# A streaming-encoder block with a retrieval layer: larger portions for the sort that runs beside the u stage, and an earlier load of the last bias row by ScalarE

## The chip, the cores and the metric

The kernel runs on one core of a Trainium2 chip. The metric is device time in microseconds. Engines: TensorE (PE), VectorE (DVE), ScalarE (ACT), GpSimd (POOL) and SyncE (SP); each works through its own queue in order. DMAs are issued by SyncE, ScalarE and GpSimd, and 16 DMA engines serve them all.

## The reference, cut to what matters

One layer over 256 positions of width 2048: adaLN modulation, a mixer (convolution and latent attention), and a retrieval layer, after which the result is scaled by a gate, added and normalised. The part around the change is the retrieval layer:

```python
scores = einsum('bshpd,hpnd->bshpn', q, sub_keys)
top_v, top_i = top_k(scores, 16)                  # per head and half
best_v, best_i = top_k(top_v[0] + top_v[1], 16)
expert = i1 * 128 + i2                            # one of 128*128 experts
gate = softmax(best_v)
act = gelu(einsum('td,tnd->tn', h, u_tab[expert])) * gate
x = x + gt_f * einsum('tn,tnd->td', act, v_tab[expert])
y = rms_norm(x)                                   # gt_f = silu(c) @ W_ada[5] + b_ada[5]
```

Each of 256 positions picks 128 of 16384 experts.

## The kernel before, in words

The first third of the program is the modulation, the mixer and the query projection. Then come two stages for the retrieval layer.

**The u stage** goes through all 16384 experts in 128 blocks of 128 (the loop `for i1 in range(NBLK)`). For a block SyncE loads 1 MB of u (`ru`, L214); ScalarE copies it to a rounded high part `hu` (L225), VectorE makes the low part `lu` as the difference (L226), and TensorE does 32 products with `hu` (L241, L242) and then 16 with `lu` (L247). There are two buffers for `hu` and `lu` and four for `ru`. ScalarE takes Gelu of the result into a tile `A` of eight blocks (L1269).

Beside it, "side" work is handed out in portions. A generator yields, after each piece of work, a number that stands for its cost; `pay(x)` adds `x` to a budget at each block and takes pieces until the budget is spent. Up to block 49 the side work is the choice of experts: one-hot products that write the gate of each expert and position to the DRAM tensor `gd`. From block 50 on it is `sort_steps`: experts of 128 at a time are sorted by which groups of positions use them. Its steps in order: a mask and two keys (VectorE, tile `work`), 24 classes, their counts (`clstot` on TensorE), prefix sums and the flag `miss`, then six times four classes: ranks (`rank`, TensorE, L1145 and L1148) and their collection (`rk`, L1133, L1138, L1140), then the place of each expert (`place`, cast at L1164). Then GpSimd issues 128 scatters (L1170), which write the experts' names to their places in DRAM (`permd`), loads them back (L1180) and casts them to `perm_idx` (L1183).

Four more things run in the u stage. Every fourth to eighth block `ask` loads the gates `gg` (L1203), `weigh` multiplies them into `A` (L1209, VectorE) and `put` stores the product to `actd` (L1213). `gtf_steps` sums the last modulation row from sixteen 1 MB loads (L1055, L1057); in block 118 `gtf_finish` adds its rows up on TensorE (`gtfp`, L1066) and adds the bias row `bt` on VectorE (L1067). Right behind it VectorE works out `half_rows` from `perm_idx` (L1315). In blocks 108 to 124 (`EARLY_AT`) GpSimd issues nine gathers of v rows by `perm_idx` (`early`, `rv`; L1238). Block 125 stores the last part of the activations.

**The tail.** GpSimd gathers v rows (1 MB each) and the activations that belong to them (`mc`, `mcs`; L1249), 109 of each, and TensorE multiplies them (`po`, L1323) in an order that `plan()` lays down; some need high and low parts (L230, L231). At the end VectorE and ScalarE scale by `gtf`, add and normalise.

What sets the order: `bt` and the `gg` tiles share a pool of two buffers (`g8`). `keep` holds an instruction in program order on its engine; elsewhere the scheduler places instructions by dependence and priority. So a piece of side work that is handed out in an earlier block stands earlier in its engine's queue.

Of the kernel before, what the change touches and what calls it, by code (L numbers as in the profile page):

```python
# [28 lines left out]
NBLK = 128  # L29
# [21 lines left out]
DEFER = (15, 16, 17, 18, 19)  # L51
SORT_FROM = 51
SORT_SIDE = 2.4
TAIL = 2
HELD = 5
AHEAD = 14
# [97 lines left out]
def hybrid_block_kernel(  # L154
# [22 lines left out]
    nc = tc.nc  # L177
    V, S, PE = nc.vector, nc.scalar, nc.tensor
# [11 lines left out]
    def ps_tile(name):  # L190
        return psp.tile([128, 512], F32, tag="ps", name=name)
# [16 lines left out]
    def keep(x):  # L208
        tc.keep_in_program_order(x)
        return x  # L210
# [6 lines left out]
    def load_split(src, name, hp=HPP, alloc=None):  # L217
        raw = load_raw(src, "r" + name)
        with tc.high_priority(offset=hp):
            if alloc is not None:  # L220
                hi, lo = alloc("h" + name), alloc("l" + name)
            else:
                hi = wp.tile([128, 2048], F32R, tag="whi", name="h" + name)
                lo = wp.tile([128, 2048], F32R, tag="wlo", name="l" + name)
            S.activation(hi, raw, AF.Copy)  # L225
            V.tensor_tensor(lo, raw, hi.bitcast(F32), ALU.subtract)  # L226
        return hi, lo
# [5 lines left out]
    def mm3(dst, w, rhs, ncx, woff=0, sets=None):  # L233
        whi, wlo = w
        rhi, rlo = rhs
        sets = sets or (tuple(range(ncx)),)
        last = sets[-1][2:] + sets[-1][:2] if isinstance(rhi, Behind) else sets[-1]
        for cs in sets:
            for c in cs:
                sl = slice((woff + c) * 128, (woff + c + 1) * 128)  # L240
                PE.matmul(dst, lhsT=whi[:, sl], rhs=rhi[:, c], start=(c == sets[0][0]), stop=False)  # L241
                PE.matmul(dst, lhsT=whi[:, sl], rhs=rlo[:, c], start=False, stop=False)  # L242
            if isinstance(rhi, Behind):
                cs = cs[2:] + cs[:2]
            for c in cs:
                sl = slice((woff + c) * 128, (woff + c + 1) * 128)
                PE.matmul(dst, lhsT=wlo[:, sl], rhs=rhi[:, c], start=False, stop=(c == cs[-1] and cs == last))  # L247
# [626 lines left out]
    def a8(name, shape=(128, 8, 256), dt=F32):  # L874
        return ap_.tile(list(shape), dt, tag="A", name=name, bufs=ABUFS)

    def g8(name, shape, dt=F32):
        return gp.tile(list(shape), dt, tag="G", name=name)
# [12 lines left out]
    def e2(name):  # L891
        return sp.tile([128, 512], F32, tag="e2", name=name, bufs=E2BUFS)
# [157 lines left out]
    def gtf_steps(acc):  # L1050
        for k in range(16):
            raw = load_raw(w_ada[3, k], f"ada5_{k}")
            yield
            if k == 0:
                keep(V.tensor_scalar(acc, raw, cact[:, 0:1], None, ALU.mult))  # L1055
            else:
                keep(V.scalar_tensor_tensor(acc, raw, cact[:, k:k + 1], acc, ALU.mult, ALU.add))  # L1057
            yield

    def gtf_finish(acc):  # L1060
        bt = g8("bt", (128, 2048))
        nc.gpsimd.dma_start(bt, b_gtf.partition_broadcast(128))
        for j in range(4):
            p = ps_tile(f"gtfp{j}")
            sl = slice(j * 512, (j + 1) * 512)
            PE.matmul(p, lhsT=ones, rhs=acc[:, sl], start=True, stop=True)  # L1066
            V.tensor_tensor(acc[:, sl], p, bt[:, sl], ALU.add)  # L1067
# [121 lines left out]
    def pay(x):  # L1189
        nonlocal budget  # L1190
        budget += x
        while budget > 0:
            st = next(side, None)
            if st is None:
                break
            budget -= st
# [4 lines left out]
    def ask(k):  # L1201
        gg = ggs[k] = g8(f"gg{k}", (128, T // TB, ABLK, TB))
        keep((S if 1 < k < NG - 1 else nc.gpsimd).dma_start(gg, gd[:, :, k * ABLK:(k + 1) * ABLK, :].rearrange("tb p i t -> p tb i t")))  # L1203

    def weigh(k, n=ABLK):
        gg = ggs.pop(k)
        av = ab[k].rearrange("p i (a t) -> p i a t", t=TB)
        gv = gg.rearrange("p a i t -> p i a t")
        keep(V.tensor_tensor(av[:, :n], av[:, :n], gv[:, :n], ALU.mult))  # L1209
        return av, gv  # L1210

    def put(k, n):
        keep((S if k else nc.gpsimd).dma_start(actd[k * ABLK * 128:(k * ABLK + n) * 128].rearrange("(i p) t -> p i t", p=128),  # L1213
                                ab[k][:, :n]))
# [27 lines left out]
    def fetch_m(m):  # L1242
        n = len(ms)
        to, at, rows = m, actd[:, :], index(ORDER[n])
        for h in range(2):
            if not need[n] >> 4 * (1 - h) & 15:
                to, at = m[:, 128 * h:128 * h + 128], actd.rearrange("r (h t) -> (r h) t", h=2)
                rows = bass.IndirectOffsetOnAxis(ap=half_rows[h][:, ORDER[n]:ORDER[n] + 1], axis=0)
        keep(nc.gpsimd.indirect_dma_start(to, None, at, rows))  # L1249
        ms.append(m)  # L1250

    def fetch_early():
        n = len(raws)
        if n == 0:
            t2.append(cst.tile([128, 2, 2048], F32, tag="T2", name="early"))
        if n < 2:
            fetch_raw("T2", t2[0][:, n])
        elif n == 7:
            fetch_raw("R", g8(f"rv{n}", (128, 2048)))
        else:  # L1260
            fetch_raw("R", a8(f"rv{n}", (128, 2048)))

    for i1 in range(NBLK):
        if i1 % ABLK == 0:
            ab.append(a8(f"A{i1}"))
        w = load_split(peer_u[i1], f"u{i1}", HPU)
        p = ps_tile(f"pu{i1}")
        mm3(p[:, :256], w, h2, 16)
        S.activation(ab[-1][:, i1 % ABLK], p[:, :256], AF.Gelu)  # L1269
        if i1 < UPART:  # L1270
            pay(SIDE)
            continue
        if i1 == UPART:
            for _ in side:
                pass
            gtf = sp.tile([128, 2048], F32, tag="tk", name="gtf")
            gts = gtf_steps(gtf)
            side = sort_steps()
            budget = 0.0
        for k in weighs.get(i1 - 1, ()):  # L1280
            if k:
                put(k, ABLK)
        for k in weighs.get(i1, ()):
            weigh(k)
            if not k:
                put(k, ABLK)
        for k in asks.get(i1, ()):
            ask(k)
        if i1 == EARLY_AT[0]:
            for _ in side:  # L1290
                pass
        if i1 in EARLY_AT:
            fetch_early()
        if i1 == NBLK - TAIL - 1:
            last = weigh(NG - 1, ABLK - TAIL)
            put(NG - 1, ABLK - TAIL)
            for k in range(4):
                pair = e2(f"mc{k}")
                m_free.extend((-1, pair[:, 256 * j:256 * j + 256]) for j in range(2))
            for _ in range(4):  # L1300
                fetch_m(m_free.pop(0)[-1])
        if i1 >= NBLK - TAIL:
            r = i1 % ABLK
            keep(V.tensor_tensor(last[0][:, r], last[0][:, r], last[1][:, r], ALU.mult))
        if i1 >= SORT_FROM:
            pay(SORT_SIDE)
        if i1 % 2 == 0:
            next(gts, None)
        if i1 == NBLK - 10:
            for _ in gts:  # L1310
                pass
            gtf_finish(gtf)
            half_rows = [x.bitcast(U32) for x in (ident, ones)]
            for h in range(2):
                keep(V.tensor_scalar(half_rows[h], perm, 2.0, float(h), ALU.mult, ALU.add))  # L1315
# [251 lines left out]
```

## Time and profile before

| what | value |
|---|---|
| time, median of 3 runs | 1705.12 us (1704.20 to 1711.65) |
| profiled execution, its time and its span | 1709.15 us, 1707.2 us |
| PE, DVE, ACT, POOL busy | 95%, 65%, 41%, 29% |
| mean granted clock of TensorE | 0.983 |
| the u stage, first `lu` product to last | 556 to 1335 us |
| scatters | 994.0 to 1261.3 us |
| DMA, mean over the span | 295 GB/s |

How to read the rows: a timeline row has the start, the duration, the engine, the line, the operation, the tile written and the tiles read, and in brackets the idle time of the engine before it with what ended it. A row of waits has who waited for whom: the total, the number of times, the longest. A row of windows has for one stretch the busy time of PE, PEld (TensorE's weight load), DVE, ACT and POOL with the instructions in brackets, then the granted clock, the DMA share and GB/s.

### The profile page before, as it was taken

How to read it: one execution, taken by the hardware profiler on the slowest of the kernel's cores; microseconds unless marked ns; L12 is line 12 of the kernel's file. 1: busy time of each engine (PE TensorE's matmuls, PEld its weight loads, DVE VectorE, ACT ScalarE, POOL GpSimd, SP SyncE). 2: the span in 40 equal slices, each digit the busy share in tenths (PEclk: the TensorE clock that was granted, in tenths of full speed). 3: DMA queues.
4: the chain of work that ended last, by engine and by line, in shares of the span. 5: the costliest groups of instructions: out<-in, count | busy, mean ns of one | idle time of the engine just before them, and what ended most of it. 6: DMA issues, size and time to landing. Idle time of an engine off the chain costs nothing. (4 is left out here: it accounts for less than half of the span.)

```text
span 1707.2 us, 29744 instructions
## 1 busy us (share of the span) xinstructions
PE 1619.5 (95%) x12787; PEld 1396.8 (82%) x12787; DVE 1113.9 (65%) x1431; ACT 706.4 (41%) x797; POOL 499.2 (29%) x359
## 2 busy tenths in 40 slices
PE   3999999999899999999999999999996999999895
PEld 2879899889899999999999999999996555544344
DVE  5778778777668989998996776665624224322136
ACT  3225557434544446645653333443332123312134
POOL 0000000000000000000000068888861687877570
PEclk9999999999999999999999999999998999999998
DMA  9996988879654456646679999999887798999893
GB/s 395 425 385 261 344 322 330 299 292 340 244 208 170 176 205 217 241 171 244 223 251 332 317 306 332 332 327 324 289 276 314 246 357 336 345 379 347 349 387 146
DMA packets 115912, 502.94 MB, mean 295 GB/s; under 512 B 13584, under 2 KB 55952, under 8 KB 60480
## 3 DMA queue, kind: packets, MB, share of 16 engines
q1 hardware_dynamic: 44784, 319.82, 50.1%
q0 software_dynamic: 25520, 130.83, 20.2%
q10 hardware_dynamic: 45472, 50.33, 8.8%
q8 instruction: 102, 1.67, 0.4%
q14 instruction: 34, 0.28, 0.0%
HBM read 463.13 MB, written 37.81 MB: 293 GB/s over the span
## 5 line engine op out<-in xcount | busy, mean ns | idle before, releaser
L241 PE MATMUL pu<-h2hi,hu 128*128 128x256 f32 x2048 | 479.9, 279 | 0.0
L225 ACT ACTIVATE hu<-ru 128x2048 fp32r<-128x2048 f32 x128 | 245.8, 1920 | 403.1 <-PE pu L242 358.9
L226 DVE TENSOR_TENSOR lu<-ru,hu 128x2048 fp32r<-128x2048 f32 x128 | 292.6, 2287 | 159.6 <-ACT hu L225 159.6
L241 PEld LDWEIGHTS pu<-h2hi,hu 128*128 128x128 f32 x2048 | 385.5, 188 | 0.2 <-issue 0.2
L247 PE MATMUL pu<-h2hi,lu 128*128 128x256 f32 x2048 | 255.7, 278 | 16.8 <-DVE lu L226 16.8
L1203 POOL DMA_DIRECT2D gg<-gd x3 | 3.7, 1233 | 904.8 <-DMA gd<-stage 889.4
L1170 POOL DMA_INDIRECT permd<-work x128 | 228.6, 1786 | 126.8 <-DVE work L1164 88.1
L247 PEld LDWEIGHTS pu<-h2hi,lu 128*128 128x128 f32 x2048 | 243.6, 189 | 17.1 <-DVE lu L226 17.1
L242 PE MATMUL pu<-h2loT3b,hu 128*128 128x256 f32 x1024 | 247.5, 278 | 0.0
L242 PE MATMUL pu<-h2loT3a,hu 128*128 128x256 f32 x1024 | 240.7, 278 | 0.0
L242 PEld LDWEIGHTS pu<-h2loT3b,hu 128*128 128x128 f32 x1024 | 192.9, 188 | 0.2 <-issue 0.2
L242 PEld LDWEIGHTS pu<-h2loT3a,hu 128*128 128x128 f32 x1024 | 192.6, 188 | 0.0
L1323 PE MATMUL po<-rv,mc 128*64 128x512 f32 (+1 forms) x368 | 128.0, 595 | 0.0
L1238 POOL DMA_INDIRECT rv<-in_peer_v_dram,perm_idx x65 | 77.7, 1196 | 48.2 <-ACT hu L225 21.6
L226 DVE TENSOR_TENSOR lwin<-rwin,hwin 128x2048 fp32r<-128x2048 f32 x33 | 75.5, 2288 | 23.8 <-ACT hwin L225 22.4
L1323 PE MATMUL po<-rv,mcs 128*32 128x512 f32 (+1 forms) x296 | 89.2, 594 | 0.0
L231 DVE TENSOR_TENSOR hwlo<-rv,hwhi 128x2048 fp32r<-128x2048 f32 x17 | 39.0, 2291 | 75.2 <-ACT hwhi L230 75.2
L225 ACT ACTIVATE hwin<-rwin 128x2048 fp32r<-128x2048 f32 x33 | 63.1, 1913 | 58.9 <-PE pin L724 26.6
L241 PE MATMUL pwin<-hhi,hwin 128*128 128x256 f32 x336 | 81.2, 286 | 0.0
L242 PE MATMUL pwin<-hlo,hwin 128*128 128x256 f32 x336 | 78.6, 278 | 0.0
L1323 PEld LDWEIGHTS po<-rv,mc 128*64 128x64 f32 (+1 forms) x368 | 36.4, 128 | 48.2 <-issue 45.8
L266 DVE SCALAR_TENSOR_TENSOR acc<-ada,cact,acc 128x2048 f32<-128x2048 f32 x30 | 70.4, 2346 | 6.4 <-DMA ada<-in_w_ada_dram 6.4
(577 smaller groups left out, 3238.6 us busy)
## 6 DMA issues: line engine op xcount, KB each, us to landing
ru<-in_peer_u_dram SPq DMA_DIRECT2D x128, 1024.0 KB, 6.0
ada<-in_w_ada_dram SPq DMA_DIRECT2D x96, 1024.0 KB, 7.1
rwin<-in_w_in_dram SPq DMA_DIRECT2D x33, 1024.0 KB, 7.0
rwout<-in_w_out_dram SPq DMA_DIRECT2D x16, 1024.0 KB, 5.6
rwq<-in_w_q_dram SPq DMA_DIRECT2D x16, 1024.0 KB, 4.9
gd<-stage ACTq DMA_DIRECT2D x16, 1024.0 KB, 5.2
actd<-A ACTq DMA_DIRECT2D x14, 1024.0 KB, 6.6
gg<-gd ACTq DMA_DIRECT2D x13, 1024.0 KB, 9.2
```

The costliest lines, as they stand in the source:

```text
L225: S.activation(hi, raw, AF.Copy)
L226: V.tensor_tensor(lo, raw, hi.bitcast(F32), ALU.subtract)
L231: V.tensor_tensor(lo, src, hi.bitcast(F32), ALU.subtract)
L241: PE.matmul(dst, lhsT=whi[:, sl], rhs=rhi[:, c], start=(c == sets[0][0]), stop=False)
L242: PE.matmul(dst, lhsT=whi[:, sl], rhs=rlo[:, c], start=False, stop=False)
L247: PE.matmul(dst, lhsT=wlo[:, sl], rhs=rhi[:, c], start=False, stop=(c == cs[-1] and cs == last))
L266: V.scalar_tensor_tensor(acc, raw, cact[:, k:k + 1], acc, ALU.mult, ALU.add)
L1170: put_one = nc.gpsimd.indirect_dma_start(permd[:, :], bass.IndirectOffsetOnAxis(ap=place[:, i:i + 1], axis=0), names[:, i:i + 1], None)
L1203: keep((S if 1 < k < NG - 1 else nc.gpsimd).dma_start(gg, gd[:, :, k * ABLK:(k + 1) * ABLK, :].rearrange("tb p i t -> p tb i t")))
L1238: keep(nc.gpsimd.indirect_dma_start(raw, None, v_rows, index(ORDER[len(raws)])))
L1323: keep(PE.matmul(po[tt * 4 + d4][row:row + size], lhsT=m[:, at * size:(at + 1) * size], rhs=raw[:, d4 * 512:(d4 + 1) * 512], start=start, ...
```

## The change

`SORT_SIDE`, the budget per block for the sort, goes from 2.4 to 3.2. The bias row `bt` is loaded in block 112 instead of block 118, and by ScalarE instead of GpSimd.

```diff
-SORT_SIDE = 2.4
+SORT_SIDE = 3.2
...
-    def gtf_finish(acc):
-        bt = g8("bt", (128, 2048))
-        nc.gpsimd.dma_start(bt, b_gtf.partition_broadcast(128))
+    def gtf_finish(acc, bt):
...
+        if i1 == NBLK - 16:
+            bt = g8("bt", (128, 2048))
+            keep(S.dma_start(bt, b_gtf.partition_broadcast(128)))
         if i1 == NBLK - 10:
             for _ in gts:
                 pass
-            gtf_finish(gtf)
+            gtf_finish(gtf, bt)
```

How this moves instructions. The first place is VectorE around the last steps of the sort; `lu` and a number is the low part of that block of u. Before:

```order
L226 TENSOR_TENSOR lu70_11111<-ru70_11108,hu70_11110 128x2048
L1133 SCALAR_TENSOR_TENSOR rk20_11166<-rank20_11038,work_5644 128x128 x4
L1138 TENSOR_REDUCE work_5644<-rk20_11166 128x128
L1140 TENSOR_TENSOR work_5644<-work_5644 128x128
L1158 CAST work_5644<-work_5644 128x128
...
L1164 CAST work_5644<-work_5644 128x128
L226 TENSOR_TENSOR lu71_11185<-ru71_11182,hu71_11184 128x2048
```

And after, from two groups of ranks earlier on:

```order
L226 TENSOR_TENSOR lu64_10759<-ru64_10756,hu64_10758 128x2048
L1138 TENSOR_TENSOR work_5644<-work_5644 128x128
L1131 SCALAR_TENSOR_TENSOR rk12_10742<-rank12_10664,work_5644 128x128 x4
L1131 SCALAR_TENSOR_TENSOR rk16_10813<-rank16_10677,work_5644 128x128
...
L226 TENSOR_TENSOR lu65_10824<-ru65_10821,hu65_10823 128x2048
L1057 SCALAR_TENSOR_TENSOR gtf_9852<-ada5_3_10683,cact_75,gtf_9852 128x2048
L1131 SCALAR_TENSOR_TENSOR rk20_10877<-rank20_10749,work_5644 128x128 x4
L1136 TENSOR_REDUCE work_5644<-rk20_10877 128x128
L226 TENSOR_TENSOR lu66_10894<-ru66_10891,hu66_10893 128x2048
...
L1162 CAST work_5644<-work_5644 128x128
L226 TENSOR_TENSOR lu67_10962<-ru67_10959,hu67_10961 128x2048
```

The last step, the cast to `place` (L1164 before, L1162 after), moved from ahead of block 71's low part to ahead of block 67's, and two groups of ranks now stand between `lu64` and `lu65`.

The second place is GpSimd between the scatters and the tail; `early` and `rv` are gathers of v rows, `gg15` is the last gates. Before:

```order
L1170 DMA permd_69<-work_5644 16384x1 x128
L1180 DMA work_5644<-permd_69 128x128
L1183 CAST perm_idx_5645<-work_5644 128x128
L1238 DMA early_13505<-in_peer_v_dram,perm_idx_5645 128x2048 x2
L1238 DMA rv2_13852<-in_peer_v_dram,perm_idx_5645 128x2048
L1238 DMA rv3_13968<-in_peer_v_dram,perm_idx_5645 128x2048
L1238 DMA rv4_14082<-in_peer_v_dram,perm_idx_5645 128x2048
L1062 DMA bt_14084<-in_b_gtf_dram 128x2048
L1238 DMA rv5_14213<-in_peer_v_dram,perm_idx_5645 128x2048
L1203 DMA gg15_14329<-gd_66 128x16x128
```

The load of `bt` is no longer there after; the rest stands as before. On ScalarE, after:

```order
L1267 ACTIVATE A112_13680<-pu112_13687 128x256
L1309 DMA bt_13738<-in_b_gtf_dram 128x2048
L225 ACTIVATE hu115_13858<-ru115_13856 128x2048
L1267 ACTIVATE A112_13680<-pu113_13746 128x256
```

The load now stands ahead of the high part of block 115, behind no GpSimd instruction.

## The prediction

> **What bounds the kernel now.** I read the page first: TensorE is busy 95% of the span, so a microsecond is lost where its row shows a hole. The rows are the span in 40 slices of 42.7 us.
>
> ```profile
> span 1707.2 us, 29744 instructions
> PE   3999999999899999999999999999996999999895
> PEclk9999999999999999999999999999998999999998
> ```
>
> Between the first slice and the last there is one deep hole, the digit 6 in slice 30 (1280 to 1323 us), and the clock dips beside it. It lies near the end of the u stage. The waits of TensorE, and those of VectorE in the same stretch, name it:
>
> ```profile
> PE pu L247 <- DVE lu L226: 15.9, 1, 15.9
> DVE gtf L1067 <- DMA bt<-in_b_gtf_dram: 26.7, 1, 26.7
> ```
>
> One wait of 15.9 us: TensorE needs the low part `lu` of a block of u, and VectorE, which makes it, stands in its own queue ahead of that for 26.7 us at the sum of `gtf` and the bias row `bt`. VectorE's timeline there (start, duration; in brackets the idle time before it and what ended it):
>
> ```profile
> 1261.13 2.29 DVE L226 TENSOR_TENSOR lu<-ru,hu 128x2048 fp32r<-128x2048 f32 x1 [3.19 <-ACT hu L225]
> 1290.08 2.48 DVE L1067 TENSOR_TENSOR gtf<-gtfp,bt 128x512 f32<-128x512 f32 x4 [26.66 <-DMA bt<-in_b_gtf_dram]
> 1292.48 0.21 DVE L1315 TENSOR_SCALAR ident<-perm_idx 128x128 uint32<-128x128 uint32 x1
> 1292.75 2.28 DVE L226 TENSOR_TENSOR lu<-ru,hu 128x2048 fp32r<-128x2048 f32 x1
> ```
>
> Why `bt` comes so late stands in GpSimd's timeline: the issue is queued behind all 128 scatters, the way back of the permutation and five gathers. (The last row is from the view of DMA issues: its last figure is the time from issue to landing.)
>
> ```profile
> 994.03 2.81 POOL L1170 DMA_INDIRECT permd<-work  x1 [88.07 <-DVE work L1164]
> 1260.34 0.96 POOL L1170 DMA_INDIRECT permd<-work  x1 [0.30 <-issue]
> 1268.80 0.28 POOL L1183 CAST perm_idx<-work 128x128 uint32<-128x128 f32 x1 [2.94 <-DMA work<-permd]
> 1269.61 1.01 POOL L1238 DMA_INDIRECT early<-in_peer_v_dram,perm_idx  x1 [0.53 <-POOL perm_idx L1183]
> 1275.58 0.60 POOL L1062 DMA_DIRECT2D bt<-in_b_gtf_dram  x1
> bt<-in_b_gtf_dram POOLq DMA_DIRECT2D x1, 1024.0 KB, 14.4
> ```
>
> Scatters run from 994.03 to 1261.30 (267 us), the permutation is ready at 1269.08, `bt` is issued at 1275.58 and lands 14.4 us later, at 1290. VectorE could have used it from 1263.4.
>
> **What the stall costs.** ScalarE makes one `hu` per block once TensorE has freed the buffer, so its starts are a clock of the blocks:
>
> ```profile
> 1268.21 1.92 ACT L225 ACTIVATE hu<-ru 128x2048 fp32r<-128x2048 f32 x1 [6.82 <-PE pu L242]
> 1273.76 1.92 ACT L225 ACTIVATE hu<-ru 128x2048 fp32r<-128x2048 f32 x1 [3.29 <-PE pu L242]
> 1295.12 1.91 ACT L225 ACTIVATE hu<-ru 128x2048 fp32r<-128x2048 f32 x1 [19.15 <-issue]
> 1303.36 1.92 ACT L225 ACTIVATE hu<-ru 128x2048 fp32r<-128x2048 f32 x1 [4.07 <-PE pu L242]
> 1308.84 1.92 ACT L225 ACTIVATE hu<-ru 128x2048 fp32r<-128x2048 f32 x1 [3.28 <-PE pu L242]
> 1292.00:1300.00 8.00, 4.91 (x23) 4.91 (x24) 8.00 (x7) 2.29 (x2) 5.21 (x3) 0.50 0.63 188
> ```
>
> The undisturbed spacing is 1308.84 - 1303.36 = 5.48 us. From 1273.76 to 1295.12 there are 21.36 us, 15.88 too many: the wait. From 1295.12 to 1303.36 there are 8.24 us, another 2.76 too many: the last row (a window; the clock is the third figure from the end) shows the granted clock at 0.50 just after the hole. Together 18.64 us. The Trainium skill (TensorE: Matmul & The Clock Gate, Part 1) says that an idle array falls to half clock and needs about 3.4 us of activity to come back; by that the return costs about 1.7 us, an estimate, and the sum would be 17.6. The half clock agrees with the row; the rows' 2.76 are used.
>
> **Part 1, the bias row.** Removed: one issue of 0.60 us on GpSimd. Added: one issue on ScalarE after block 112's Gelu, ahead of `hu` of block 115. An issue of the same kind there takes 0.37 us, and ScalarE idles 3 us or more before each `hu`, so it is free; if that cover went, it would cost 0.37 us. The issue could also hold ScalarE up, were its buffer not free; the two buffers of that pool are held by `gg` tiles, whose users are
>
> ```profile
> 1197.58 2.29 DVE L1209 TENSOR_TENSOR A<-A,gg 128x2048 f32<-128x2048 f32 x1
> 1224.98 2.29 DVE L1209 TENSOR_TENSOR A<-A,gg 128x2048 f32<-128x2048 f32 x1
> 1244.57 0.37 ACTq L1203 DMA_DIRECT2D gg<-gd  x1
> ```
>
> The new `bt` takes the buffer freed by the first (1199.9) and is issued shortly before `hu115`, five blocks before 1259.2 (part 3), so at 1229 to 1232; `gg14` (last row) then takes the buffer freed by the second (1227.3) and is issued at 1244.57. Margins of 29 and 17 us: no wait. With the 14.4 us of the old landing `bt` is there by 1246, 17 us before VectorE asks at 1263.4.
>
> What is late next? The two products with `perm_idx` (L1315) stand directly behind in VectorE's queue. Even with the permutation as late as now (1269.08), `lu` behind them would be done at 1269.08 + 0.28 + 2.28 = 1271.6, while TensorE first needs it at 1295.03 - 15.9 = 1279.1. So moving `bt` alone pays for the whole hole.
>
> **Part 2, the portions of the sort.** The order of VectorE puts the last step of the sort (the cast to `place`) ahead of `lu67` where it stood ahead of `lu71`. `hu67` began at 966.98, the first row here (the others serve the price, below):
>
> ```profile
> 966.98 1.92 ACT L225 ACTIVATE hu<-ru 128x2048 fp32r<-128x2048 f32 x1 [3.90 <-PE pu L242]
> 978.51 1.92 ACT L225 ACTIVATE hu<-ru 128x2048 fp32r<-128x2048 f32 x1 [3.28 <-PE pu L242]
> 984.61 1.92 ACT L225 ACTIVATE hu<-ru 128x2048 fp32r<-128x2048 f32 x1 [3.90 <-PE pu L242]
> 936.32 0.18 DVE L1111 COPY work<-clstot 128x24 f32<-128x24 f32 x1
> 938.80 0.15 DVE L1126 CAST miss<-work 128x1 int32<-128x1 f32 x1
> 982.65 2.28 DVE L226 TENSOR_TENSOR lu<-ru,hu 128x2048 fp32r<-128x2048 f32 x1
> 984.86 1.12 DVE L1133 SCALAR_TENSOR_TENSOR rk<-rank,work 128x128 f32<-128x128 f32 x4
> 987.32 2.28 DVE L226 TENSOR_TENSOR lu<-ru,hu 128x2048 fp32r<-128x2048 f32 x1
> ```
>
> So the scatters can start at about 966.98 + 1.92 + 2 for two rank products that now come earlier and some lag = 971, 23 us sooner. With the same 267 us they end at 1238, and the permutation is there at 1246, ahead of the 1263.4 where VectorE asks. That by itself would have `bt` issued at 1252.5 in the old order and landed at 1267, `lu` done by about 1272: also before 1279.1. Each part alone closes the hole, and the gains must not be added.
>
> The price is a denser VectorE at blocks 60 to 66: a group of four `rk` with its reduction and sum takes 987.32 - 984.86 = 2.46 us, and ahead of `lu65` now stand two of them, ahead of `lu66` one and a `gtf` step (as wide as a `lu`). Per block of 5.48 us (984.61 - 978.51 = 6.1 with rank products on TensorE) one `lu` (2.2) and two groups are 7.1 us, so I reckon `lu65`, `lu66` and `lu67` late by 2 to 4 us. The trace shows 2.2 us of lateness (982.65 against the end of its `hu` at 980.43) without a wait. The room: `hu` begins when TensorE has finished the high part two blocks earlier, `lu` is needed two blocks after that, so 2 x 5.48 - 1.92 - 2.29 = 6.75 us. 4 is below it: no stall. If the sum were 3 us off, a short wait of some tenths would show.
>
> SyncE now reads `miss` ahead of the load `ru63`, which waits for `lu59`; the steps from `clstot` to `miss` stand directly behind `lu59` and take 2.6 us (936.32 to 938.95): at most that, of the lead of 17.7 us worked out below.
>
> **Part 3, what now runs side by side.** This cover is gone: the first gathers ran while TensorE stood still, and now they run beside the loads of u.
>
> ```profile
> 1276.00:1284.00 8.00, 3.21 (x29) 3.01 (x27) 0.00 (x0) 0.00 (x0) 1.16 (x2) 0.96 1.01 416
> 1306.00:1312.00 6.00, 6.00 (x55) 6.00 (x54) 2.81 (x2) 2.20 (x2) 0.00 (x0) 1.00 1.02 421
> DMA to landing us min/median/max: 5.1/10.1/11.4
> 1237.26 1.92 ACT L225 ACTIVATE hu<-ru 128x2048 fp32r<-128x2048 f32 x1 [3.28 <-PE pu L242]
> 1239.21 2.29 DVE L226 TENSOR_TENSOR lu<-ru,hu 128x2048 fp32r<-128x2048 f32 x1 [3.19 <-ACT hu L225]
> ```
>
> The last figure of a window is GB/s: about 420 at full DMA. The loads of u need 1.05 MB per 5.48 us, 191 GB/s, less than half. The third row is the landing of `ru` between 1262 and 1310, beside two gathers: 11.4 us at most. A load is issued when the `lu` four blocks back is done (1239.21 + 2.29 = 1241.5) and used when its `hu` starts (1237.26 + 4 x 5.48 = 1259.2): a lead of 17.7 us. So 6.3 us are left. I take 0 here and keep 0 to 8 us for the range.
>
> By the Trainium skill (DMA: Bandwidth & Descriptors, Queues, rings and completion order) each DMA engine takes turns between the queues that have work. With two queues that leaves u 210 GB/s and agrees with the 11.4 us; with a third, ScalarE's, 140, and a load of 7.5 us instead of 5. I count that in the second case.
>
> **Part 4, does the rest move along?** The tail begins on GpSimd with the first gather of `mc`, which waits for the last store of the gated activations:
>
> ```profile
> 1325.75 0.37 ACTq L1213 DMA_DIRECT2D actd<-A  x1
> 1333.25 0.99 POOL L1249 DMA_INDIRECT mc<-actd,perm_idx  x1 [8.39 <-DMA actd<-A]
> 1400.00:1500.00 100.00, 100.00 (x454) 52.56 (x453) 37.47 (x29) 32.11 (x30) 77.47 (x60) 1.00 0.90 346
> ```
>
> That store hangs on block 125, so it comes 18.64 us sooner. In the tail TensorE is 100% busy, GpSimd's queue close to full (77.5 us and 60 gaps of the 0.30 seen before a scatter) and DMA at 0.90; whichever of the three sets the pace, all start from that store, and the whole tail shifts. The nine early gathers come 23 us sooner, the end of the u stage 18.6 us sooner: the stock at the tail's start isn't worse.
>
> **Sum.** -18.64 (hole and clock) + 0 (issue) + 0 (VectorE) + 0 (DMA). The profiled execution took 1709.15 us, 1.95 more than its span; by it 1690.5. It is 4.0 us above the median of 1705.12 shown; by the median 1686.5, which I forecast. The runs shown, 1704.20 to 1711.65, less 18.64 give 1685.6 to 1693.0; the other way some waits of the tail may shrink by 3 us, so this case runs from 1682 to 1694.
>
> **The rivals.**
> - *Crowded DMA, most of the gain kept.* Gathers, `bt` or `gg14` and u loads together push a load or two past its 17.7 us; TensorE waits some 2 to 6 us and pays 2.76 for the clock. For it: 421 GB/s is a full fabric. Against: the 11.4 us. 1686.5 + 5 to 11: 1691 to 1697.
> - *The tail doesn't move.* If DMA or GpSimd work through a fixed amount that began before the store, the end stays: 1705. For it: DMA at 0.90 throughout. Against: the 8.39 us for which GpSimd stood idle at the head of the tail, waiting for exactly that store.
> - *Slower: the loads of u starve.* Place: from the permutation (1246) on, the last seven or so blocks whose loads are still to come. It decides from a landing beyond 17.7 us on: if u gets 140 GB/s throughout, a block lasts 7.5 us, and each short hole brings the half clock: 2.0 + 2.76 = 4.8 us, seven times 33, less 18.6: about 1720. Against it: two queues, not three, for most of that time.
> - *The change doesn't do what it says.* If the scatters start no sooner, `bt` on ScalarE alone still closes the hole, so the time is the forecast's; no case of its own.
>
> **How the numbers follow.** A measurement of this kernel can tell about 0.5% (8.5 us) from no change. Forecast 0.70, crowded DMA 0.14, unmoved tail 0.10, starved loads 0.06. Faster: 0.70 + 0.14 = 0.84; same 0.10; slower 0.06. The range takes the first case's 1682 and the second's 1697, with a microsecond or two for each: 1681 to 1699.
>
> **What would show it.** In the changed profile: the wait of `pu` for `lu` near 1279 and VectorE's wait for `bt` gone, PEclk without the dip in slice 29 or 30; scatters from 970 to 1240; first gathers at 1246; `hu` at 5.48 us throughout the last blocks; the tail's first `mc` near 1315, and the stretch from there to the end unchanged at 374 us. I am wrong if the hole closes and that stretch grows by as much, if new waits for `ru` stand between 1246 and 1290, or if `pu` waits for `lu` at blocks 65 to 67.

## The result, and the profile after

The changed kernel takes 1686.28 us (median of 4 runs, 1684.03 to 1687.71), the kernel before 1706.45 us beside it (4 runs, 1704.20 to 1711.65): a ratio of 0.9876, with a 95% interval of 0.9849 to 0.9903. The forecast was 1686.5. The profiled execution took 1687.52 us with a span of 1685.7 us, 21.5 us shorter than the span before.

The span in 40 slices no longer has the digit 6 in slice 30, and the clock has no dip there:

```profile
PE   3999999999999999999999999999999999999895
PEclk8999999999999999999999999999999999999998
```

VectorE's timeline after, at the place where it stood for 26.7 us (start, duration, and in brackets the idle time before). The sum with `bt` now follows the `lu` ahead of it without a gap, and so do the two products with the permutation:

```profile
1259.35 2.29 DVE L226 TENSOR_TENSOR lu<-ru,hu 128x2048 fp32r<-128x2048 f32 x1 [3.19 <-ACT hu L225]
1261.55 2.47 DVE L1065 TENSOR_TENSOR gtf<-gtfp,bt 128x512 f32<-128x512 f32 x4
1263.95 0.22 DVE L1316 TENSOR_SCALAR ident<-perm_idx 128x128 uint32<-128x128 uint32 x1
1268.37 2.29 DVE L226 TENSOR_TENSOR lu<-ru,hu 128x2048 fp32r<-128x2048 f32 x1 [4.07 <-ACT hu L225]
```

ScalarE's timeline after: the issue of `bt`, and the starts of `hu`, which are the clock of the blocks:

```profile
1226.34 0.35 ACTq L1309 DMA_DIRECT2D bt<-in_b_gtf_dram  x1
...
1266.42 1.92 ACT L225 ACTIVATE hu<-ru 128x2048 fp32r<-128x2048 f32 x1 [6.82 <-PE pu L242]
1271.97 1.92 ACT L225 ACTIVATE hu<-ru 128x2048 fp32r<-128x2048 f32 x1 [3.29 <-PE pu L242]
1277.45 1.92 ACT L225 ACTIVATE hu<-ru 128x2048 fp32r<-128x2048 f32 x1 [3.28 <-PE pu L242]
...
1288.41 1.92 ACT L225 ACTIVATE hu<-ru 128x2048 fp32r<-128x2048 f32 x1 [3.28 <-PE pu L242]
```

From the first `hu` of these to the last there are 1288.41 - 1266.42 = 21.99 us, where before there were 1308.84 - 1268.21 = 40.63: the difference is 18.64 us. The span's 21.5 us are these 18.64, 1.79 us that were there already at the first of these rows (1268.21 against 1266.42), and 1.64 of these already at an `hu` of 591.16 against 589.52, some 300 us ahead of the first instruction that the change moves, so I count them to the spread between executions, and 1.0 us in the tail (from the first `mc` to the end there were 373.9 us, and now 372.9).

GpSimd's timeline after, with the first and the last scatter, the way back of the permutation, the first gather, and the first gather of the tail:

```profile
969.21 2.89 POOL L1168 DMA_INDIRECT permd<-work  x1 [64.19 <-DVE work L1162]
...
1237.90 2.65 POOL L1168 DMA_INDIRECT permd<-work  x1 [0.30 <-issue]
1246.76 0.59 POOL L1178 DMA_DIRECT2D work<-permd  x1 [6.21 <-PE pu L242]
1252.33 0.29 POOL L1181 CAST perm_idx<-work 128x128 uint32<-128x128 f32 x1 [4.98 <-DMA work<-permd]
1253.15 1.00 POOL L1236 DMA_INDIRECT early<-in_peer_v_dram,perm_idx  x1 [0.54 <-POOL perm_idx L1181]
...
1312.82 0.99 POOL L1247 DMA_INDIRECT mc<-actd,perm_idx  x1 [8.40 <-DMA actd<-A]
```

Here is the one thing that is not as forecast. The scatters begin 24.8 us sooner (994.03 before), but they end only 20.7 us sooner (1240.55 against 1261.30), and the permutation is cast only 16.5 us sooner (1268.80 before). Part of what the sort gained is lost on the way. The experiments found where.

### The profile page after: what moved, and what is told of

Read it like the earlier page. It is cut to its first block, busy times and chain, and to the rows that moved or that the text cites. A ratio compares the mean times of both kernels' runs of the same rounds, so it can differ in the third digit from the quotient of the medians.

```text
span 1685.7 us, 29738 instructions
## 1 busy us (share of the span) xinstructions
PE 1615.6 (96%) x12782; PEld 1396.0 (83%) x12787; DVE 1113.9 (66%) x1431; ACT 706.7 (42%) x797; POOL 503.0 (30%) x358
## 5 line engine op out<-in xcount | busy, mean ns | idle before, releaser
L1168 POOL DMA_INDIRECT permd<-work x128 | 232.6, 1818 | 102.9 <-DVE work L1162 64.2
```

What stands on the lines that cost most here:

```text
L1168: put_one = nc.gpsimd.indirect_dma_start(permd[:, :], bass.IndirectOffsetOnAxis(ap=place[:, i:i + 1], axis=0), names[:, i:i + 1], None)
```

## The experiments

Two theories go in. **Mine:** the time gained is the hole of `bt` and the clock behind it; either part of the change closes it. **The rival:** the gain needs the scatters and gathers to start sooner (they run ahead of the tail), or only one part matters. Each ratio below is to the kernel before on the same chip, with its 95% interval.

**The bias row alone.** The old portions of the sort, `bt` by ScalarE at block 112.

```
 SORT_SIDE = 2.4
-        nc.gpsimd.dma_start(bt, b_gtf.partition_broadcast(128))
...
+        if i1 == NBLK - 16:
+            bt = g8("bt", (128, 2048))
+            keep(S.dma_start(bt, b_gtf.partition_broadcast(128)))
```

> The kernel of before with the bias row alone loaded by ScalarE at block 112; the sort keeps its old portions, so the scatters still run to about 1261 and perm is cast at about 1269. Theory (the whole gain is the hole of the bias row, 15.9 us of TensorE and 2.76 us of half clock behind it): TensorE has no wait for lu near 1280, VectorE waits some 5 to 8 us for perm without anybody waiting for it, and the time is 1685 to 1689, a ratio of about 0.988. Rival (the gain needs the earlier scatters and gathers): the u loads now start with less lead, the first hu after perm waits for them, and the time stays between 1692 and 1706, a ratio above 0.991.

Measured: 1688.71 us, ratio 0.9911 (0.9885 to 0.9938), whose interval overlaps with that of the full change (0.9849 to 0.9903). TensorE has no wait for `lu` there. VectorE's timeline of this run:

```profile
1264.42 2.48 DVE L1065 TENSOR_TENSOR gtf<-gtfp,bt 128x512 f32<-128x512 f32 x4
1269.90 0.23 DVE L1316 TENSOR_SCALAR ident<-perm_idx 128x128 uint32<-128x128 uint32 x1 [3.00 <-POOL perm_idx L1181]
1271.23 2.29 DVE L226 TENSOR_TENSOR lu<-ru,hu 128x2048 fp32r<-128x2048 f32 x1 [0.97 <-ACT hu L225]
```

VectorE waits 3.00 us for the permutation, less than the 5 to 8 expected, and still waits for `hu` after it: nobody is late. From the `hu` at 1269.29 to the end of the span (1688.5) there are 419.2 us; in the changed kernel 419.3 (1685.7 - 1266.42), before 439.0 (1707.2 - 1268.21). So by the traces the bias row by itself brings the whole gain. The medians fell by 15.6 us here and by 20.2 us with the full change, each beside its own runs of the kernel before, so they don't exclude that the portions add a few microseconds.

**The engine of the bias row alone.** The old place in the program, block 118, and the old portions; ScalarE issues it.

```
-        nc.gpsimd.dma_start(bt, b_gtf.partition_broadcast(128))
+        S.dma_start(bt, b_gtf.partition_broadcast(128))
```

> The kernel of before with the engine that issues the bias row alone changed: ScalarE issues it at the old place in the program, block 118, and not GpSimd; the portions are the old ones. Theory (the row was late because of the queue that it stood in, and not because of its place in the program): issued near 1246, landed near 1255 to 1261, before VectorE asks for it at about 1263; no hole, 1685 to 1689. Rival (the six blocks of lead are needed): the row lands behind 1266, TensorE waits 2 us or more and gets the half clock, 1690 or more.

Measured: 1688.09 us, ratio 0.9901 (0.9870 to 0.9932). The row was issued at 1245.0 and landed 12.3 us later, ahead of the sum that starts at 1263.3; VectorE does not wait for it. The issue itself, right behind that of a load of gates, took 2.42 us of ScalarE's time, which stayed within ScalarE's idle time ahead of the next `hu`. So it was the queue that made the row late, not the place in the program.

**The portions alone.** The kernel before with the new number; `bt` stays on GpSimd.

```
-SORT_SIDE = 2.4
+SORT_SIDE = 3.2
```

> The kernel of before with the larger portions alone; the bias row is still issued by GpSimd behind the scatters, perm and the gathers. Theory as in the prediction (the earlier scatters close the hole by themselves: the row is issued at 1252.5 and lands at 1267): 1685 to 1689. Theory with the times that the changed kernel showed (perm not before 1252.6, the row issued near 1262.7, landed near 1277, lu done near 1282 where it is needed near 1277.4): a rest of the hole of 4.7 us and the clock's 2.76 us, 1692 to 1695. Rival (the portions give nothing): 1703 to 1707.

Measured: 1695.04 us, ratio 0.9943 (0.9925 to 0.9962): half of the gain. My step in the prediction falls, and the middle theory holds: its time is at the upper edge of that range (1692 to 1695), with a wait of 6.1 us where 4.7 was expected. The trace is of the slowest of the ten executions (1700.19 us). GpSimd's and VectorE's timelines of this run, and the wait of TensorE (us in total, times, longest):

```profile
1255.13 0.29 POOL L1183 CAST perm_idx<-work 128x128 uint32<-128x128 f32 x1 [5.28 <-DMA work<-permd]
1265.14 0.60 POOL L1062 DMA_DIRECT2D bt<-in_b_gtf_dram  x1
```

```profile
1281.19 2.48 DVE L1067 TENSOR_TENSOR gtf<-gtfp,bt 128x512 f32<-128x512 f32 x4 [16.86 <-DMA bt<-in_b_gtf_dram]
```

```profile
PE pu L247 <- DVE lu L226: 6.1, 1, 6.1
```

The row is issued at 1265.14 where the prediction had 1252.5, and there at 1281.2 where it had 1267. Of the 12.6 us by which the issue is late, 9.4 are the permutation (1255.42 against 1246) and 3.2 the five gathers ahead of it, which took 9.7 us from the permutation on and not 6.5: two of them (2.41 and 2.69 us in place of 0.94) stood still beside a `lu`, as the scatters do below. The spacing of `hu` behind the wait (1286.22 to 1294.66, 8.44 us) adds 2.96 for the clock: 9.0 us are left of the hole's 18.64.

**Smaller portions.** The other direction, to see whether the hole is as long as the row is late.

```
-SORT_SIDE = 2.4
+SORT_SIDE = 2.0
```

> The kernel of before with smaller portions, 2.0 us for a block and not 2.4: the place of the scatters moves back by five blocks, 27.4 us, and all of GpSimd's work to the bias row with it. Theory (the hole is as long as the row is late, one for one; the clock's return costs the same 2.76 us whatever the length): TensorE waits about 43 us in place of 15.9, and the time is 1730 to 1736. Rival (what runs ahead in a hole is given back later: loads and expert weights are further on when TensorE resumes): the wait is as long, but part of it comes back, 1712 to 1726.

Measured: 1717.58 us, ratio 1.0080 (1.0053 to 1.0107). The time lies in the rival's range, but not for the rival's reason. GpSimd's timeline, then the waits:

```profile
1017.59 1.03 POOL L1170 DMA_INDIRECT permd<-work  x1 [109.93 <-DVE work L1164]
...
1280.64 0.28 POOL L1183 CAST perm_idx<-work 128x128 uint32<-128x128 f32 x1 [1.55 <-DMA work<-permd]
...
1287.41 0.60 POOL L1062 DMA_DIRECT2D bt<-in_b_gtf_dram  x1
```

```profile
DVE gtf L1067 <- DMA bt<-in_b_gtf_dram: 37.4, 1, 37.4
PE pu L247 <- DVE lu L226: 26.7, 1, 26.7
```

The scatters begin 23.6 us later than before, but the row is issued only 11.8 us later, and TensorE's wait is 10.8 us longer. Nothing is given back behind the hole: from the `hu` of 1267.94 to the end there are 448.7 us, 29.4 more than in the changed kernel, and wait and clock (`hu` at 1273.50, 1305.63, 1313.71, 1319.26) are 29.3. The hole costs one for one; what is not one for one is the scatters and the way back. The stretch of the 128 scatters shrinks when they start later: 271 us in the changed kernel, 267 before, 259 here. And from the end of the last scatter to the permutation there are 12.1, 7.8 and 4.3 us, while the DMA engines were busy for 0.98, 0.57 and 0.08 of that time: in the changed kernel loads of u, a store of activations and a load of gates run there, here hardly anything else is moved. The order fits a way back that gets slower beside other transfers; no run tests this alone.

**What sets the pace of the scatters.** GpSimd's and VectorE's timelines of the changed kernel over the same 12 us:

```profile
999.73 1.90 POOL L1168 DMA_INDIRECT permd<-work  x1 [0.30 <-issue]
1001.94 1.96 POOL L1168 DMA_INDIRECT permd<-work  x1 [0.30 <-issue]
1004.20 1.90 POOL L1168 DMA_INDIRECT permd<-work  x1 [0.30 <-issue]
1006.40 0.96 POOL L1168 DMA_INDIRECT permd<-work  x1 [0.30 <-issue]
1007.66 2.73 POOL L1168 DMA_INDIRECT permd<-work  x1 [0.31 <-issue]
```

```profile
998.51 2.29 DVE L1207 TENSOR_TENSOR A<-A,gg 128x2048 f32<-128x2048 f32 x1
1000.72 2.35 DVE L1057 SCALAR_TENSOR_TENSOR gtf<-ada,cact,gtf 128x2048 f32<-128x2048 f32 x1
1002.98 2.28 DVE L226 TENSOR_TENSOR lu<-ru,hu 128x2048 fp32r<-128x2048 f32 x1
1007.27 2.29 DVE L226 TENSOR_TENSOR lu<-ru,hu 128x2048 fp32r<-128x2048 f32 x1 [2.00 <-ACT hu L225]
```

The scatter of 1006.40 begins while VectorE is idle and takes 0.96 us. The one of 1001.94 begins during the `gtf` step, which ends at 1003.07, and is done 0.83 us behind that, at 1003.90; the one of 1007.66 waits for the `lu` that ends at 1009.56 and is done at 1010.39, again 0.83 behind it. All 128 rows go this way, before and after: 55 scatters of the changed kernel took 0.96 us, and 73 began during an operation of VectorE and ended 0.83 to 0.90 us after it. So the stretch is 128 x (0.96 + 0.30) = 161 us and 110 more, 1.5 us for each of the 73. The Trainium skill (SBUF — State Buffer, Who interferes with whom) has a rule for it: VectorE and GpSimd share a port, and an operation of VectorE with two operands in SBUF shuts out an instruction of GpSimd that reads SBUF until it is done, while a reduction does not. The rows agree with the first half; two kernels test the cause. Both leave the gate row uncomputed, and so out of the result.

```
-  keep(V.scalar_tensor_tensor(acc, raw, cact[:, k:k + 1], acc, ALU.mult, ALU.add))
+  pass
```

```
-  keep(V.scalar_tensor_tensor(acc, raw, cact[:, k:k + 1], acc, ALU.mult, ALU.add))
+  keep(V.tensor_reduce(acc[:, k:k + 1], raw, AX.X, ALU.add))
```

> The changed kernel without the fifteen additions at L1057 by which VectorE gathers the gate row (the gate is left out of the result). In the changed kernel 73 of the 128 scatters began during an operation of VectorE, and each of these ended 0.8 to 0.9 us after that operation; the 55 others took 0.96 us. Theory (a scatter stands still while VectorE works on two SBUF operands): without the additions the scatters' stretch falls from 271 us to about 252, the last one ends near 1221 in place of 1240.6, perm is cast near 1233 in place of 1252.3, and the time stays at 1684 to 1689, since nobody waits for perm. Rival (a scatter's length comes from its own descriptors and the DMA queue): the stretch stays at 268 to 273.

> The changed kernel with the fifteen additions at L1057 replaced by fifteen reductions of the same 128x2048 tile to one column (the gate is not computed), which read one SBUF operand in place of two and take VectorE about as long. Theory (only an operation with two SBUF operands holds the scatters up): the stretch is as without the additions, about 252 us, perm near 1233. Rival (any operation of VectorE of this length holds them up): 268 to 273 us as in the changed kernel, perm near 1252. The time stays at 1684 to 1689 in both.

Measured: without the additions the scatters run from 965.37 to 1219.42, 254 us, and with the reductions from 970.24 to 1222.24, 252 us; the permutation is cast at 1227.9 and 1232.5. With the reductions VectorE is as busy as before, and yet 12 of 12 scatters that began during one took 0.96 us. One such pair, VectorE and GpSimd:

```profile
1001.80 2.28 DVE L1057 TENSOR_REDUCE gtf<-ada 128x1 f32<-128x2048 f32 x1
```

```profile
1003.03 0.96 POOL L1168 DMA_INDIRECT permd<-work  x1 [0.30 <-issue]
```

So it is neither the descriptors nor the DMA queue nor VectorE's time that holds a scatter up. One difference is left: a reduction not only reads one operand fewer, it also writes one column and not 2048. The kernel before has, in its tail, an operation that writes wide rows but has only one operand in SBUF, since `po` lies in PSUM. VectorE, then GpSimd:

```profile
1674.16 1.29 DVE L1454 TENSOR_TENSOR rv<-po,gtf 128x512 f32<-128x512 f32 x2 [1.14 <-PEq L1433]
1675.37 2.28 DVE L231 TENSOR_TENSOR hwlo<-rv,hwhi 128x2048 fp32r<-128x2048 f32 x1
```

```profile
1674.22 0.94 POOL L1238 DMA_INDIRECT rvg<-in_peer_v_dram,perm_idx  x1 [11.28 <-PEq L1433]
1675.46 3.00 POOL L1249 DMA_INDIRECT mcs<-actd,ones  x1 [0.30 <-issue]
```

The gather that begins with the `po` operation takes 0.94 us; the next, during a difference of two SBUF tiles, takes 3.00 and ends 0.81 behind it. In all traces ten gathers began during a `po` operation with 0.34 us or more of it to go, and all ten took 0.94 to 0.95. These are gathers and the rows have 512 columns, but wide writing alone holds nothing up there; what is left is operations with two operands in SBUF. The times, 1689.77 and 1684.01 us, are of one run each, the first just above the 1684 to 1689 expected; both traces also have a new wait of TensorE (2.6 us near 1284, and 3.8 us near 1286), of the kind that comes next.

**The portions alone, without the additions.** If the scatters' pace is why the portions alone did not do it, a faster pace must do it.

```
-SORT_SIDE = 2.4
+SORT_SIDE = 3.2
-  keep(V.scalar_tensor_tensor(acc, raw, cact[:, k:k + 1], acc, ALU.mult, ALU.add))
+  pass
```

> The kernel with the larger portions alone (the bias row still issued by GpSimd behind perm and the gathers), without the fifteen additions at L1057 (the gate row is left out of the result). With them, in the run of the portions alone, the scatters took 271 us, the row was issued at 1265.1, and TensorE waited 6.1 us and got the half clock. Theory (the scatters are held up by VectorE's operations with two SBUF operands, and this is why the portions alone did not close the hole): the stretch falls to about 253 us, perm comes near 1235, the row is issued near 1245 and lands ahead of 1268; no wait for lu, 1683 to 1690. Rival (the row is late for its own long landing, 14 to 16 us, or for the gathers ahead of it that wait for buffers): a wait of 3 us or more stays, 1691 to 1696.

Measured: 1694.99 us (1689.37 to 1698.37, 5 runs), ratio 0.9933 (0.9906 to 0.9961). Half of the theory shows: the row is issued at 1235.5, and VectorE adds it at 1260.7 without a wait. But the time does not fall, for a wait of another kind takes its place. VectorE's timeline 20 us further on, and a window behind it (the granted clock is the third figure from the end):

```profile
1280.78 2.29 DVE L1209 TENSOR_TENSOR A<-A,gg 128x2048 f32<-128x2048 f32 x1 [10.96 <-DMA gg<-gd]
```

```profile
1285.00:1293.00 8.00, 7.67 (x43) 7.68 (x44) 4.77 (x3) 2.29 (x2) 1.08 (x1) 0.62 0.84 313
```

VectorE waits 10.96 us for the gates of the last group but one, the `lu` behind that is late, TensorE waits 3.3 us (`hu` from 1276.61 to 1285.35) and gets the low clock, 2.96 us. This trace is the fastest of the five executions, so how long the wait was in the others is not known.

**Larger portions, and the gates.** The changed kernel with twice the portion; then the same with that one load of gates four blocks sooner, ahead of the gathers (the second pair of lines).

```
-SORT_SIDE = 3.2
+SORT_SIDE = 6.4
-  asks.setdefault(at - (6 if 1 < k < NG - 1 else 3), []).append(k)
+  asks.setdefault(at - (10 if k == NG - 2 else 6 if 1 < k < NG - 1 else 3), []).append(k)
```

> The changed kernel with portions of 6.4 us in place of 3.2: the place of the scatters comes some 20 us sooner once more, and GpSimd's own store and load still stand ahead of them. Theory (VectorE's lead of 6.75 us is not used up, since lu ran only 1.0 to 1.5 us late with 3.2): no wait, 1683 to 1688, perm some 12 us sooner than in the changed kernel without anybody asking for it. Rival (the lead is used up): one wait for lu of about 2 us near block 62 and the half clock behind it, 1688 to 1692.

> The kernel with portions of 6.4 us, and beside it the load of gg for the last but one group of A asked for four blocks sooner, near 1219 in place of 1241.3, so that it stands ahead of the gathers, which began at 1225 there. In the run with 6.4 us this load landed 37 us after its issue, VectorE waited 9.3 us for it, three lu were late behind that, and TensorE waited 1.6 us. Theory (six gathers of 1 MB that start ahead of the load hold it back on the DMA engines): it lands within 12 us, VectorE does not wait for it, TensorE has no wait for lu near 1280, and the time falls by about 2 us to 1685 to 1690. Rival (the load was late for something else, its buffer or ScalarE's queue): VectorE still waits 5 us or more for it, and TensorE 1 us or more.

Measured: with 6.4 alone 1690.30 us, ratio 0.9902 (0.9872 to 0.9932); the time lies in the rival's range, but the rival's wait is not there. The first group of rows is of this run: the first gather (GpSimd), the sum that waits for the gates (VectorE), and the load of the gates in the view of DMA issues (its last figure is the us to landing). The second is VectorE's and ScalarE's rows of the run with the sooner load.

```profile
1225.12 3.04 POOL L1236 DMA_INDIRECT early<-in_peer_v_dram,perm_idx  x1 [0.53 <-POOL perm_idx L1181]
1278.49 2.29 DVE L1207 TENSOR_TENSOR A<-A,gg 128x2048 f32<-128x2048 f32 x1 [9.31 <-DMA gg<-gd]
gg<-gd ACTq DMA_DIRECT2D x1, 1024.0 KB, 37.1
```

```profile
1221.17 0.37 ACTq L1201 DMA_DIRECT2D gg<-gd  x1
1270.89 2.28 DVE L1207 TENSOR_TENSOR A<-A,gg 128x2048 f32<-128x2048 f32 x1
```

VectorE's lead was not used up by 6.4: `lu` was 4.1 us late at most (block 61), and there is no wait in the sort. The cost is at the other end. Gathers that start at 1225 stand ahead of the load issued at 1241.29, which then lands after 37.1 us; in the changed kernel, whose gathers start at 1253.15, the same load lands in 7.2 us. TensorE waits 1.6 us. Asked for at 1221, ahead of the gathers, the load is there in time (its landing is not in the trace), and neither VectorE nor TensorE waits. So the order of load and gathers is what counts, as in the theory. How the gathers hold the load back is not shown in full. On ScalarE's own queue a store of activations stands ahead of it, issued at 1235.81 behind the first gathers and landed only 28.05 us later (5.73 in the changed kernel), while the loads of u on SyncE's queue land in 7.5 to 10.8 us beside the same gathers. From 1241 to 1278 SyncE's queue moved 6.37 MB in 890 packets, GpSimd's 5.42 in 885 and ScalarE's 2.05 in 3062, so it is the queue with the small packets that falls behind. The gain itself is too small to see: the second kernel took 1714.03 us on a chip where the one before took 1726.13, a ratio of 0.9910 (0.9871 to 0.9949).

**Portions without limit.** The changed kernel with 20 us per block; then the same with two DMAs of GpSimd given to ScalarE (the other lines).

```
-SORT_SIDE = 3.2
+SORT_SIDE = 20.0
-  keep((S if 1 < k < NG - 1 else nc.gpsimd).dma_start(gg, ...
+  keep((S if 0 < k < NG - 1 else nc.gpsimd).dma_start(gg, ...
-  keep((S if k else nc.gpsimd).dma_start(actd[...
+  keep(S.dma_start(actd[...
```

> The changed kernel with portions of 20 us for each block in place of 3.2: the sort's steps are handed out within a few blocks, and its place comes ahead of the lu of block 60. Theory (VectorE's lead of 6.75 us absorbs a lateness of lu and no more): lu runs late by up to some 10 us, TensorE waits 2 to 5 us in blocks 52 to 62 and gets the half clock's 2.8 us behind it; 1689 to 1695 where the changed kernel has 1686.3. Rival (the lead is wider than I read it, since TensorE's block itself gets longer by the rank matmuls): no new wait, 1684 to 1688. Scatters begin some 30 us before those of the changed kernel in both.

> The kernel with portions of 20 us, and beside it two DMAs that GpSimd issued there moved to ScalarE: the store of the first group of A and the load of gg for the second group. In the run with 20 us, 16 and then 56 scatters stood ahead of these two in GpSimd's queue, the store went out at 957 and the load at 1015, and TensorE waited 13.5 and 39.0 us. Theory (these two DMAs behind the scatters are the whole loss): both holes go, and the time is 1685 to 1692, of which up to 5 us for VectorE's lateness in the sort. Rival (the loss comes from VectorE's own load by the sort's steps in few blocks): the holes stay in size, 1720 or more.

Measured: with 20 us alone 1741.30 us, ratio 1.0220 (1.0193 to 1.0248), far outside of both theories. TensorE's waits and GpSimd's timeline:

```profile
PE pu L247 <- DVE lu L226: 39.8, 2, 39.0
PE pu L241 <- ACT hu L225: 13.5, 1, 13.5
```

```profile
957.21 0.94 POOL L1211 DMA_DIRECT2D actd<-A  x1
...
1014.99 1.21 POOL L1201 DMA_DIRECT2D gg<-gd  x1
```

In the changed kernel both DMAs are issued ahead of the first scatter; here 16 and 56 scatters stand ahead of them. It is the old fault in another place: a load that others need, behind scatters on GpSimd. With both on ScalarE the holes of 39.0 and 13.5 us go, and the time is 1695.58 us, ratio 0.9940 (0.9912 to 0.9967). That is above the 1685 to 1692 expected. What is left in its trace is a wait of 6.2 us for `lu` at 936 to 942, and one of 1.2 us near 1290. Both stand behind a wait of VectorE for gates (8.00 and 8.87 us): ScalarE, which itself waited 5.7 us for a load of u there, issued the first of them at 916.42. So even with 20 us I have no run in which VectorE's own work alone fills its lead.

**More on the DMA engines.** Four copies of 1 MB that the result does not use.

```
+  spare = drp.tile([4, 128, 2048], F32, name="spare")
...
+  if i1 in (113, 114, 115, 116):
+      keep(S.dma_start(spare[i1 - 113], peer_u[i1 - 100]))
```

> The changed kernel with four extra copies of 1 MB each from DRAM to DRAM, of no use to the result, on ScalarE's queue at blocks 113 to 116, so that the DMA engines have more to carry just ahead of the gathers and beside the bias row. Theory (a u load is asked for 17.7 us ahead of its use, and landed in 10.0 us at most): the loads land later, in 12 to 17 us, nobody waits, 1685 to 1689. Rival (crowded DMA, as priced in the prediction): hu waits for ru by 2 us or more, and the half clock comes on top, 1690 to 1697.

Measured: 1683.38 us, ratio 0.9883 (0.9866 to 0.9900), as fast as the changed kernel. The landing of `ru` between 1225 and 1300 (min, median, max), first in the changed kernel, then with the copies:

```profile
DMA to landing us min/median/max: 4.9/7.5/10.0
```

```profile
DMA to landing us min/median/max: 6.5/10.1/14.9
```

The loads do come later, up to 14.9 us, and still inside their lead of 17.7. TensorE does wait once, 2.0 us, but not for `ru`: the third copy held ScalarE for 10.40 us at its issue (1243.65; the first two took 0.6), and `hu` came late behind it.

## Why the prediction was right, and the step that was not

- **The hole and the clock, 18.64 us.** Right to the hundredth in the profiled pair. That the median came within 0.2 us of 1686.5 is luck beyond that: the kernel before measured 1.3 us more than in the runs shown, and the medians fell by 20.2 us, 1.5 more than the sum. The runs with longer and shorter holes give the same law: 6.1, 15.9 and 26.7 us of wait cost 9.0, 18.6 and 29.3 us of time.
- **Part 1.** Right. The row was issued at 1226.34 (a little ahead of the 1229 to 1232 forecast), landed in 8.2 us without ScalarE waiting, and alone brought the gain.
- **Part 2, its size and its claim.** This step failed: "with the same 267 us they end at 1238, and the permutation is there at 1246", and so "each part alone closes the hole". The start was right (969.2 against 971), the rest late: 1240.55 and 1252.6, since the stretch took 4 us longer than the 267, and the way back from the last scatter to the permutation 12 us in place of 8, beside more loads than before. In the old order the five gathers ahead of `bt` took 3.2 us longer as well. The portions alone left 9.0 us. The scatters' length is no constant: they stand still for each of VectorE's two-operand operations, and moved sooner they meet more of them (73 held up, 70 before, 64 with portions of 2.0), because late scatters find VectorE with less to do: before, the 11 that began from 1240 on took 1.42 us in the mean, where the stretches of 40 us ahead had 1.7 to 2.0, and with portions of 2.0 there were 22 that began there, of 1.27 us, the last of them while VectorE itself stood waiting for `bt`. It did no harm in the sum, since Part 1 had already paid for the hole.
- **Part 2, its price.** No wait, as forecast, but sized too high: `lu65` was 1.0 us late, `lu66` 1.5 (964.81 against an end of `hu` at 963.32) and `lu67` 0.0, where I had 2 to 4. With two rank groups TensorE's own blocks are longer there, too. Twice the portion, with 4.1 us of lateness, does not fill the room of 6.75 us either; where it ends the runs did not show, as with 20 us other waits came first.
- **Part 3.** Right: 10.0 us at most, and 14.9 with 4 MB more. I had the right rival at the wrong place: what a crowded DMA delays first is not a load of u but the gates on ScalarE's queue, and that once the gathers start 25 to 28 us sooner than in the changed kernel; there, at 1253, they come behind the load of 1242.78. Nor do the queues share as I reckoned (210 GB/s for u with two queues, 140 with three): with three at work in the run with 6.4, u got 172 GB/s, the gathers 146 and ScalarE's queue 55 in the mean over those 37 us. And the price of this rival, 5 to 11 us, fits one wait only up to 9 (6 + 2.76).
- **Part 4.** Right: the first `mc` at 1312.82 (near 1315 forecast), and from there to the end 372.9 us against 374.0. Over all kernels this stretch lay between 365.5 and 375.6, and at 403.5 in the last one with portions of 6.4, on the slower chip, without a rule that I found; that stays open.

Of the two parts, the larger portions bring nothing that the traces show once the row is on ScalarE; alone they bring half.

## What to carry to other kernels

When one engine waits for a load, look what stands ahead of the load's issue in its queue before moving any work: another queue (0.35 us on ScalarE) did what 22 us of earlier scatters could not. Don't shift a stretch of GpSimd's DMA work as a block of fixed length; count VectorE's two-operand operations beside it. A place in a queue can be too early as well as too late: when long work on GpSimd comes sooner, ask which loads it now passes.

## What the runs showed of the hardware that I had not expected

- A scatter that GpSimd issues takes 0.96 us alone and up to 3.11 beside VectorE. In the 14 traces 930 scatters began during a VectorE operation with two operands in SBUF, and 929 of them ended 0.83 to 0.90 us after it; the one other began 0.03 us behind the operation's start and took 1.00 us. A reduction of 2.28 us does not delay a scatter.
- TensorE lost nothing of its clock behind waits of 1.6 and 2.0 us (granted clock 1.00, and 0.3 us more in the blocks behind), and got the half clock with waits of 2.6 us and more. A window behind the wait of 2.6 us (without the additions, 1282.42 to 1285.06; the clock is the third figure from the end):

```profile
1285.00:1288.41 3.41, 3.35 (x15) 3.35 (x16) 2.21 (x2) 1.91 (x1) 0.82 (x1) 0.50 0.65 226
```

- What the return costs depends on how long the half clock stays on behind the wait, not on the length of the wait: behind 2.6, 3.8, 3.3, 6.1, 15.9 and 26.7 us of waiting it stayed for 3.35, 3.41, 5.82, 5.78, 5.40 and 4.83 us, and the blocks there were 1.8, 2.0, 2.96, 2.96, 2.76 and 2.67 us longer, a little over half of it.
- An issue on ScalarE mostly takes 0.33 to 0.6 us. It held the engine for 10.40 us when it was the third copy of 1 MB between places in DRAM within 12 us on its queue, with a store and a load of gates between them; with portions of 20 us two stores held it for 6.85 and 5.63 us. What it waits for there no run tests.
